# A two-layer decoder on one core: weight chunks split 1024 columns at a time, head outputs kept in DRAM

## The chip, the core and the metric

The kernel runs on one NeuronCore of a Trainium2 chip, as one program. The metric is the device time of one execution in microseconds, as the median of several runs. The core's engines are TensorE (PE in the profile, its weight loads PEld), VectorE (DVE), ScalarE (ACT), GpSimd (POOL) and SyncE (SP). Each works through its own instructions in a fixed order and waits on semaphores for the others. Here SP, ScalarE and POOL also issue DMA transfers, each on its own queue.

## The reference

Two pre-norm residual layers over 512 tokens of 2048 features, all in float32. Layer 0 projects its normed input to 12288 columns, runs two recurrences (RG-LRU, 8 heads of 256; HGRN2, 16 heads of 128), gates both, and maps the 4096 joined features back to 2048. Layer 1 is differential attention with 8 heads (two causal softmax maps each), again between two projections.

```python
h = rms_norm(x, rec_norm)
rg_x, rg_g, hg_q, hg_f, hg_i, hg_g = split(h @ rec_w_in)       # 2048 -> 6 x 2048
y_a = rg_lru(conv(rg_x), ...) * silu(rg_g)
y_b = rms_norm(hgrn2(silu(hg_q), hg_f, hg_i), hg_out_norm) * silu(hg_g)
x = x + concat(y_a, y_b) @ rec_w_out                           # 4096 -> 2048
h = rms_norm(x, att_norm)
q, k, v, g = split(h @ att_w_in)                               # 2048 -> 4 x 2048
o = rms_norm(diff_attention(rope(rms_norm(q)), rope(rms_norm(k)), v, lam))
x = x + (o * (1 - lam_init) * silu(g)) @ att_w_out             # 2048 -> 2048
```

## The kernel before, in words

**Products.** TensorE multiplies in a float32r format that holds only part of a float32. So each operand is split exactly into a high part (a rounding copy) and a low part (the rest), and each product is made as three: high·high, high·low, low·high (`mm3`, L104 to L106 before). A product takes 128 x 128 weights against 512 moving columns.

**Weights.** They come in chunks of [128, 1024] float32 (512 KB): 192 of `w_rec`, 8 of `w_gate`, 64 of `w_rout`, 128 of `w_att`, 32 of `w_aout`. `raw` loads a chunk into one of three buffers `wraw` on SP's queue (L84). `split` makes `whi` with a ScalarE cast (L91) and `wlo` with a VectorE subtract (L92), 512 columns at a time, in five buffers each. Splits have high priority in the scheduler, which otherwise orders each engine's instructions by data flow. A chunk feeds 24 products of 512 columns.

**Stages.** `proj_feat` projects 256 features per job (4 chunks, two PSUM banks `pj` out of four), `proj_tok` 512 features per job (four banks). First come the HGRN2 jobs, two heads at a time, then the RG-LRU jobs, then the output projection (4 blocks of 16 chunks, HGRN2's y16 to y31 first and y0 to y15 after them), then attention (4 pairs of heads, with jobs q, k, v, g of 8 chunks each) and the last output projection (4 blocks of 8 chunks). The heads' own work is written as generators, and `tick` takes some steps of it between two half chunks of a projection.

**Head outputs.** They stay in SBUF as tiles `yb0` to `yb7`, `ya0` to `ya15` and, in layer 1, `y0` to `y15`. For each block of the output projections `jit_split` splits each of them anew, 512 columns at a time, in the same `whi` and `wlo`.

**Start.** `run` loads x transposed in eight pairs of tiles into `yb0` to `yb7` on SP's queue, three weight chunks among them; ScalarE and VectorE make `h0h`, `h0l` and so on from them (L744, L745). `prepare` loads x again in eight tiles on POOL's queue (L165), in turns through `yb5`, `yb6`, `yb7`, and ScalarE squares them and sums the squares (L166). From the sums comes 1/rms of each token, which TensorE turns into a row (`pm<-cst,xr`, L182) that ScalarE copies to `rrow` (L183). VectorE multiplies each finished projection bank by it (`hin<-pj,rrow`, L384), which frees the bank.

Of the kernel before, what the change touches and what calls it, by code (L numbers as in the profile page):

```python
# [9 lines left out]
F32 = mybir.dt.float32  # L10
# [9 lines left out]
P = 128  # L20
# [15 lines left out]
# steps of the heads' own work between two half chunks of a projection  # L36
# [10 lines left out]
# columns of the packed constants  # L47
# [4 lines left out]
class Kernel:  # L52
# [27 lines left out]
    def raw(self, src):  # L80
        if self.raws and self.use_raws:
            return self.raws.pop(0)
        t = self.wp.tile([P, CH], F32, name="wraw", bufs=3)
        self.nc.sync.dma_start(t, src)  # L84
# [23 lines left out]
    def rsqrt(self, pool, ss, n, scale, eps):  # L108
        """(ss * scale + eps) ** -0.5 on a few columns"""
# [7 lines left out]
        # first guess from the bits, then Newton until float32 has converged  # L117
# [8 lines left out]
    def proj_feat(self, h, src, chunk0, ticks):  # L126
        """256 output features as two [feature, token] banks"""
        ps = [self.pj.tile([P, S], F32, name="pj") for _ in range(2)]
        for c in range(4):
            raw = self.raw(src[chunk0 + c])  # L130
            for s in range(2):
                w = self.split(raw[:, s * HALF:(s + 1) * HALF])
                for kk in range(2):
                    kt = 4 * c + 2 * s + kk
                    for o in range(2):
                        sl = slice(kk * 256 + o * P, kk * 256 + (o + 1) * P)
# [4 lines left out]
    def proj_tok(self, lhs, order, src, chunk0, ticks):  # L141
        """512 output features as four [token, feature] banks; lhs(kt) gives the split activations"""
        ps = [self.pj.tile([P, S], F32, name="pj") for _ in range(NT)]
        n = len(order)
        for c in range(n // 2):
            raw = self.raw(src[chunk0 + c])
            for s in range(2):
                i = 2 * c + s
                w = self.split(raw[:, s * HALF:(s + 1) * HALF])
# [7 lines left out]
    def prepare(self):  # L157
        """1 / rms of each token, as columns and as a row repeated for every partition; small constants"""
# [3 lines left out]
        for i in range(8):  # L162
            xt = self.ybp.tile([P, 2 * S], F32, name=f"yb{5 + i % 3}")
# [47 lines left out]
        # the scale of q goes with k  # L211
# [709 lines left out]
```

## Time and profile before

| | |
|---|---|
| median of 3 runs | 2596.66 us (2596.36 to 2597.73) |
| profiled execution: span from the first to the last instruction | 2594.6 us |
| mean granted TensorE clock | 0.998 |
| L91 casts, 128x512, of weight chunks | x848, mean 618 ns |
| L92 subtracts, 128x512, of weight chunks | x848, mean 688 ns |
| HBM read, written | 239.95 MB, 8.39 MB |

The span of the profiled execution lies 2.06 us under the median of the runs; a device time of its own is not listed for it. In a row of groups, "out<-in" names tiles, "x" a count; a bracket [t <-X] in a timeline says that the engine was idle for t us and that X ended it. An instruction's time is from its start to its modelled end, so back-to-back products, which start some 0.225 us apart, show as 0.39 us each.

### The profile page before, as it was taken

The numbers are of one execution on the slowest core, as the hardware profiler recorded it, in microseconds if no ns is written. First come the engines' busy times: TensorE is split into PE (matmuls) and PEld (weight loads), VectorE is DVE, ScalarE is ACT, GpSimd is POOL, SyncE is SP. The second block draws the span as 40 slices with busy tenths as digits, with TensorE's granted clock in tenths as the row PEclk, the third lists the DMA queues.
The fourth block names the chain that finished last, engine by engine and source line by source line (L and its number), as shares of the span: only waits on it lengthen the run. The fifth ranks groups of instructions, "written<-read, shape, count | busy, mean of one in ns | idle before, by whom it ended". The sixth has DMA issues, their size and how long they took to land.

```text
span 2594.6 us, 33221 instructions
## 1 busy us (share of the span) xinstructions
PE 2579.6 (99%) x12416; PEld 2126.2 (82%) x12416; DVE 1417.0 (55%) x3073; ACT 1258.6 (49%) x2458; POOL 4.6 (0%) x12
## 2 busy tenths in 40 slices
PE   9999999999999999999999999999999999999999
PEld 7888888888888888888888888888888888888887
DVE  5466557646646665545654555344544534544654
ACT  8445545535444455556544444334434434534543
POOL 0000000000000000000000000000000000000000
PEclk9999999999999999999999999999999999999999
DMA  6222222222222222222232333222222222222243
GB/s 244 96 74 82 81 82 74 81 90 74 76 95 74 74 98 102 97 93 98 90 128 95 127 130 120 98 98 75 81 97 77 79 91 82 76 95 93 86 146 114
DMA packets 73457, 250.48 MB, mean 97 GB/s; under 512 B 8144, under 2 KB 8656, under 8 KB 73296
## 3 DMA queue, kind: packets, MB, share of 16 engines
q1 hardware_dynamic: 71712, 243.58, 26.8%
q0 software_dynamic: 1152, 4.19, 0.4%
q8 instruction: 97, 1.59, 0.2%
q10 hardware_dynamic: 432, 0.59, 0.1%
q14 instruction: 64, 0.52, 0.1%
HBM read 239.95 MB, written 8.39 MB: 96 GB/s over the span
## 4 chain that ended last, share of the span: by engine, by line
PE 94%; DVE 2%; ACT 2%; DMA 1%; issue 1%; SPq 0%; ACTq 0%
PE pj L104 28%; PE pj L106 28%; PE pj L105 28%; PE pm L258 2%; PE pm L570 1%; PE pm L104 1%; PE pm L106 1%; PE pm L105 1%; PE pm L343 1%; PE pm L554 1%; DMA yb<-in_x 0%; PE pm L332 0%; PE pm L345 0%; ACT a L675 0%; PE pm L359 0%
## 5 line engine op out<-in xcount | busy, mean ns | idle before, releaser
L92 DVE TENSOR_TENSOR wlo<-wraw,whi 128x512 fp32r<-128x512 f32 x848 | 582.3, 688 | 671.4 <-ACT whi L91 641.2
L91 ACT CAST whi<-wraw 128x512 fp32r<-128x512 f32 x848 | 523.0, 618 | 765.0 <-PE pj L106 463.7
L106 PE MATMUL pj<-whi,wlo 128*128 128x512 f32 x768 | 299.6, 390 | 0.0
L105 PE MATMUL pj<-wlo,whi 128*128 128x512 f32 x768 | 299.4, 390 | 0.0
L104 PE MATMUL pj<-whi 128*128 128x512 f32 x768 | 299.3, 390 | 0.0
L106 PEld LDWEIGHTS pj<-whi,wlo 128*128 128x128 f32 x768 | 144.2, 188 | 30.5 <-DVE wlo L92 0.6
L104 PEld LDWEIGHTS pj<-whi 128*128 128x128 f32 x768 | 144.2, 188 | 30.4 <-issue 0.5
L105 PEld LDWEIGHTS pj<-wlo,whi 128*128 128x128 f32 x768 | 144.2, 188 | 29.1
L240 ACT ACTIVATE e<-e 128x512 f32<-128x512 f32 x80 | 50.5, 632 | 131.7 <-DVE e L239 97.6
L92 DVE TENSOR_TENSOR wlo<-ya,whi 128x512 fp32r<-128x512 f32 x64 | 44.3, 693 | 89.9 <-ACT whi L91 89.9
L92 DVE TENSOR_TENSOR wlo<-y,whi 128x512 fp32r<-128x512 f32 x64 | 44.2, 691 | 82.3 <-ACT whi L91 82.3
L91 ACT CAST whi<-ya 128x512 fp32r<-128x512 f32 x64 | 39.7, 621 | 100.9 <-PE pj L105 100.9
L91 ACT CAST whi<-y 128x512 fp32r<-128x512 f32 x64 | 39.9, 623 | 94.1 <-PE pj L105 90.2
L92 DVE TENSOR_TENSOR wlo<-yb,whi 128x512 fp32r<-128x512 f32 x64 | 44.1, 690 | 72.2 <-ACT whi L91 72.0
L91 ACT CAST whi<-yb 128x512 fp32r<-128x512 f32 x64 | 39.8, 621 | 76.5 <-PE pj L105 76.5
L258 PEld LDWEIGHTS pm<-e 128*128 128x128 f32 x512 | 66.6, 191 | 5.0 <-DVE e L241 0.3
L258 PE MATMUL pm<-e 128*128 128x128 f32 x512 | 67.5, 275 | 0.0
L241 DVE TENSOR_TENSOR e<-e,hin 128x256 f32<-128x256 f32 x80 | 33.6, 420 | 58.8 <-ACT e L240 58.8
L575 ACT ACTIVATE p<-pm,mx 128x128 f32<-128x128 f32 (+3 forms) x64 | 33.7, 526 | 40.6 <-DVE mx L573 38.6
L572 DVE TENSOR_REDUCE mx<-pm 128x1 f32<-128x128 f32 (+3 forms) x64 | 30.4, 485 | 32.6 <-PE pm L571 32.3
L675 ACT ACTIVATE a<-pj,rstd 128x128 f32<-128x128 f32 x128 | 47.3, 421 | 0.3
L104 PE MATMUL pj<-h0h,whi 128*128 128x512 f32 x80 | 33.8, 423 | 5.2 <-DVE hin L384 2.9
(474 smaller groups left out, 6483.0 us busy)
## 6 DMA issues: line engine op xcount, KB each, us to landing
wraw<-in_w_rec SPq DMA_DIRECT2D x192, 512.0 KB, 3.2
wraw<-in_w_att SPq DMA_DIRECT2D x128, 512.0 KB, 3.2
wraw<-in_w_rout SPq DMA_DIRECT2D x64, 512.0 KB, 3.2
wraw<-in_w_aout SPq DMA_DIRECT2D x32, 512.0 KB, 3.2
yb<-in_xT SPq DMA_DIRECT2D x8, 512.0 KB, 8.5
yb<-in_x POOLq DMA_DIRECT2D x8, 512.0 KB, 5.5
wraw<-in_w_gate SPq DMA_DIRECT2D x8, 512.0 KB, 3.2
xo<-in_x SPq DMA_DIRECT2D x16, 256.0 KB, 4.0
```

What stands on the lines that cost most here:

```text
L91: self.nc.scalar.copy(hi, src)
L92: self.nc.vector.tensor_tensor(lo, src, hi.bitcast(F32), op=ALU.subtract)
L104: mm(out, a[0], b[0], start=start, stop=False)
L105: mm(out, a[0], b[1], start=False, stop=False)
L106: mm(out, a[1], b[0], start=False, stop=stop)
L240: nc.scalar.activation(e, e, AF.Exp)
L241: V.tensor_tensor(e1, e1, vw(qs, h)[:, :, 1, :], op=ALU.mult)
L258: nc.tensor.matmul(ps[:, sl], e[:, sl], e[:, sl], start=True, stop=True)
L343: nc.tensor.matmul(po[:, sl], st[:, sl], v[:, t, vc:vc + P], start=True, stop=t == 0)
L572: V.tensor_reduce(mx[:, i:i + 1], ps[:, :n], axis=AX.X, op=ALU.max)
L575: nc.scalar.activation(e[:, :n], ps[:, :n], AF.Exp, scale=ATT_SCALE, bias=mx[:, i:i + 1], accum_out=z[:, i:i + 1])
L675: nc.scalar.activation(x[:, t, g * P:(g + 1) * P], ps[t][:, g * P:(g + 1) * P], AF.Square, scale=r1, accum_out=ss[:, t * 4 + g:t * 4 + g + 1])
```

## The change

Weight chunks are split whole, 1024 columns by one cast and one subtract. The split tiles double in size, with three buffers (`WBUFS`) in place of five, and raw chunks have two (`RBUFS`) in place of three. Head outputs are written as pairs of feature tiles [128, 2, 512] to DRAM by a DMA on ScalarE's queue (`keep_y`), and each block of an output projection reads each pair back on SP's queue (`y_split`), splits it 1024 columns wide, and uses the two halves. The tiles of `yb` become one name with eight buffers that are taken in turn, by `prepare` as well. At the start two weight chunks are loaded among the x tiles instead of three. The scratch tile `jk3` becomes bfloat16. Comments and docstrings are dropped, so line numbers move a little. Core of the diff:

```diff
+RBUFS, WBUFS, YBUFS = 2, 3, 2
...
-        t = self.wp.tile([P, CH], F32, name="wraw", bufs=3)
+        t = self.wp.tile([P, CH], F32, name="wraw", bufs=RBUFS)
...
-    def split(self, src):
-        hi = self.wp.tile([P, HALF], F32R, name="whi", bufs=5)
-        lo = self.wp.tile([P, HALF], F32R, name="wlo", bufs=5)
+    def split(self, src, pool, name, bufs):
+        hi = pool.tile([P, CH], F32R, name=name + "hi", bufs=bufs)
+        lo = pool.tile([P, CH], F32R, name=name + "lo", bufs=bufs)
...
-            raw = self.raw(src[chunk0 + c])
+            wh, wl = self.split(self.raw(src[chunk0 + c]), self.wp, "w", WBUFS)
             for s in range(2):
                 i = 2 * c + s
-                w = self.split(raw[:, s * HALF:(s + 1) * HALF])
+                w = [x[:, s * HALF:(s + 1) * HALF] for x in (wh, wl)]
...
-            xt = self.ybp.tile([P, 2 * S], F32, name=f"yb{5 + i % 3}")
+            xt = self.ybp.tile([P, 2 * S], F32, name="yb", bufs=8)
...
-        self.y[16 + hd] = y
+        if hd % 2:
+            self.keep_y(8 + hd // 2, self.yb)
...
-                y = self.y1p.tile([P, S], F32, name=f"y{kt}")
-                nc.scalar.activation(y, ps, AF.Identity, scale=self.gsub[:, fb:fb + 1])
-                self.y[kt] = y
+                if fb == 0:
+                    y = self.y1p.tile([P, 2, S], F32, name="ya", bufs=2)
+                nc.scalar.activation(y[:, fb, :], ps, AF.Identity, scale=self.gsub[:, fb:fb + 1])
+                if fb:
+                    self.keep_y(2 * pr + hh, y)
...
-    def jit_split(self, kt):
-        return self.split(self.y[kt])
+    def keep_y(self, i, y):
+        d = self.dr.tile([P, 2 * S], F32, name=f"yd{i}")
+        self.nc.scalar.dma_start(d, y.rearrange("p a c -> p (a c)"))
+        self.y[i] = d
+
+    def y_split(self):
+        at = [None, None]
+        def lhs(kt):
+            i = kt // 2
+            if at[0] != i:
+                if i not in self.y:
+                    self.drain()
+                t = self.yp.tile([P, CH], F32, name="yraw", bufs=2)
+                self.nc.sync.dma_start(t, self.y[i])
+                at[:] = i, self.split(t, self.yp, "y", YBUFS)
+            sl = slice(kt % 2 * S, (kt % 2 + 1) * S)
+            return at[1][0][:, sl], at[1][1][:, sl]
+        return lhs
...
-                if i % 2 == 0 and i < 6:
+                if i % 2 == 0 and i < 2 * RBUFS:
                     self.raws.append(self.raw(self.w_rec[i // 2]))
...
-                ps = self.proj_tok(lhs, order, self.w_rout, 16 * n, 1)
+                ps = self.proj_tok(self.y_split(), order, self.w_rout, 16 * n, 1)
```

At the start of the program SP issued its loads like this before; the third `wraw` is the third weight chunk, and the eight `yb` loads are the pairs of x tiles:

```order
L730 DMA yb_132<-in_xT 128x1024
L734 DMA col<-in_col 128x163
L84 DMA wraw<-in_w_rec 128x1024
L730 DMA yb_138<-in_xT 128x1024
L730 DMA yb_140<-in_xT 128x1024
L84 DMA wraw<-in_w_rec 128x1024
L730 DMA yb_144<-in_xT 128x1024
L730 DMA yb_146<-in_xT 128x1024
L84 DMA wraw<-in_w_rec 128x1024
L730 DMA yb_150<-in_xT 128x1024
```

And like this now, with equal rows counted:

```order
L756 DMA yb<-in_xT 128x1024
L760 DMA col<-in_col 128x163
L86 DMA wraw<-in_w_rec 128x1024
L756 DMA yb<-in_xT 128x1024 x2
L86 DMA wraw<-in_w_rec 128x1024
L756 DMA yb<-in_xT 128x1024 x5
L764 DMA cst<-in_cst 128x384
L86 DMA wraw<-in_w_rec 128x1024 x135
```

The third weight chunk has moved from between the fifth and the sixth pair of x tiles to behind the eighth and the constants.

On ScalarE the casts of that chunk stood between the h tiles before (h8h is the first tile that needs it):

```order
L744 ACTIVATE h8h<-yb_146,col 128x512
L744 ACTIVATE h9h<-yb_146,col 128x512
L91 CAST whi<-wraw 128x512 x2
L744 ACTIVATE h10h<-yb_150,col 128x512
L744 ACTIVATE h11h<-yb_150,col 128x512
```

Now its one cast stands behind the last of them, ahead of the first square of x:

```order
L770 ACTIVATE h12h<-yb,col 128x512
L770 ACTIVATE h13h<-yb,col 128x512
L206 ACT_TABLE_LOAD
L770 ACTIVATE h14h<-yb,col 128x512
L770 ACTIVATE h15h<-yb,col 128x512
L93 CAST whi<-wraw 128x1024
L167 ACTIVATE yb,ss_336<-yb 128x1024
```

At the end of the attention, ScalarE before: `pm` holds the transposes of the last head, y14 and y15 are its outputs, and the casts of y12 to y15 are the last of the first block:

```order
L91 CAST whi_20669<-wraw_20667 128x512
L626 ACTIVATE y14_20596<-pm_20591,gsub_527 128x512
L626 ACTIVATE y15_20603<-pm_20598,gsub_527 128x512
L91 CAST whi_20673<-y12_20383 128x512
L91 CAST whi_20689<-wraw_20667 128x512
L91 CAST whi_20693<-y13_20390 128x512
L91 CAST whi_20711<-wraw_20709 128x512
L91 CAST whi_20715<-y14_20596 128x512
```

And now: `ya_18916` is the pair of the last head, `yd7` its place in DRAM, `yraw_19016` what comes back of it:

```order
L93 CAST yhi_18982<-yraw_18980 128x1024
L93 CAST whi_19012<-wraw_19010 128x1024
L632 ACTIVATE ya_18916<-pm_18911,gsub_495 128x512
L632 ACTIVATE ya_18916<-pm_18918,gsub_495 128x512
L704 DMA yd7_18924<-ya_18916 128x1024
L93 CAST whi_19065<-wraw_19063 128x1024
L93 CAST yhi_19018<-yraw_19016 128x1024
```

A store and a load have come between the last head's outputs and their cast.

More of the change, by code (lines that the diff above doesn't have):

```diff
@@ L129, in proj_feat @@
         for c in range(4):
-            raw = self.raw(src[chunk0 + c])
+            w = self.split(self.raw(src[chunk0 + c]), self.wp, "w", WBUFS)
             for s in range(2):
-                w = self.split(raw[:, s * HALF:(s + 1) * HALF])
                 for kk in range(2):
@@ L135, in proj_feat @@
                     for o in range(2):
-                        sl = slice(kk * 256 + o * P, kk * 256 + (o + 1) * P)
+                        sl = slice(s * HALF + kk * 256 + o * P, s * HALF + kk * 256 + (o + 1) * P)
                         self.mm3(ps[o], (w[0][:, sl], w[1][:, sl]), h[kt], kt == 0, kt == KD - 1)
@@ L145, in proj_tok @@
         for c in range(n // 2):
-            raw = self.raw(src[chunk0 + c])
+            wh, wl = self.split(self.raw(src[chunk0 + c]), self.wp, "w", WBUFS)
             for s in range(2):
                 i = 2 * c + s
-                w = self.split(raw[:, s * HALF:(s + 1) * HALF])
+                w = [x[:, s * HALF:(s + 1) * HALF] for x in (wh, wl)]
                 a = lhs(order[i])
@@ L360, in hgrn_head @@
         if hd % 2 == 0:
-            self.yb = self.ybp.tile([P, 2, S], F32, name=f"yb{hd // 2}")
+            self.yb = self.ybp.tile([P, 2, S], F32, name="yb", bufs=8)
         y = self.yb[:, hd % 2, :]
         V.scalar_tensor_tensor(y, ps, self.col[:, C_HGN:C_HGN + 1], sg, op0=ALU.mult, op1=ALU.mult)
-        self.y[16 + hd] = y
+        if hd % 2:
+            self.keep_y(8 + hd // 2, self.yb)
         yield
@@ L448, in rg_head @@
             xs.append((hi, lo))
-            w.append(self.split(wg[:, ct * HALF:(ct + 1) * HALF]))
+            if ct == 0:
+                wh, wl = self.split(wg, self.wp, "w", WBUFS)
+            w.append([x[:, ct * HALF:(ct + 1) * HALF] for x in (wh, wl)])
             yield
@@ L487, in rg_head @@
             V.tensor_tensor_scan(m, a[jt], m, 0.0, op0=ALU.mult, op1=ALU.add)
-            y = self.yap.tile([P, S], F32, name=f"ya{c}")
-            V.tensor_tensor(y, m, sg[jt], op=ALU.mult)
-            self.y[c] = y
+            if jt == 0:
+                y = self.yap.tile([P, 2, S], F32, name="ya", bufs=2)
+            V.tensor_tensor(y[:, jt, :], m, sg[jt], op=ALU.mult)
+            if jt:
+                self.keep_y(hd, y)
             yield
@@ L728, in run @@
             for i in range(8):
-                t = self.ybp.tile([P, 2, S], F32, name=f"yb{i}")
+                t = self.ybp.tile([P, 2, S], F32, name="yb", bufs=8)
                 nc.sync.dma_start(t, self.xT[:, 2 * i:2 * i + 2, :])
@@ L761, in run @@
             self.rk = pool(st, "rk")
+            self.yp = pool(st, "yp")
             self.mids.append(m)
@@ L770, in run @@
             for n in range(4):
-                def lhs(kt):
-                    if kt not in self.y:
-                        self.drain()
-                    return self.jit_split(kt)
-                ps = self.proj_tok(lhs, order, self.w_rout, 16 * n, 1)
+                ps = self.proj_tok(self.y_split(), order, self.w_rout, 16 * n, 1)
                 xo = []
@@ L781, in run @@
                     nc.sync.dma_start(x1d[t, n], o)
-                    jk = self.ev.tile([P, S], F32, name="jk3", bufs=1)
+                    jk = self.ev.tile([P, S], BF16, name="jk3", bufs=1)
                     nc.scalar.activation(jk, o, AF.Square, accum_out=ss1[:, t, n:n + 1])
@@ L816, in run @@
             V.tensor_scalar(self.nlam, self.nlam, -LAM_INIT, None, op0=ALU.add)
+            self.yp = pool(st, "yp")
             self.attention(h1)
             for n in range(4):
-                def lhs(kt):
-                    if kt not in self.y:
-                        self.drain()
-                    return self.jit_split(kt)
-                ps = self.proj_tok(lhs, list(range(KD)), self.w_aout, 8 * n, TICK_OUT)
+                ps = self.proj_tok(self.y_split(), list(range(KD)), self.w_aout, 8 * n, TICK_OUT)
                 xo = self.ak.tile([P, NT, S], F32, name="a0")
```

1 line of the change is left out of this document (removed).

## The prediction

> **What bounds the kernel now.** I read the busy times and the chain that ended last first, then TensorE's waits, then windows by stage, and at last the timeline of the first 60 us. In the rows of busy times each engine has its microseconds, its share of the span and its instructions.
>
> ```profile
> span 2594.6 us, 33221 instructions
> PE 2579.6 (99%) x12416; PEld 2126.2 (82%) x12416; DVE 1417.0 (55%) x3073; ACT 1258.6 (49%) x2458; POOL 4.6 (0%) x12
> ...
> PE 94%; DVE 2%; ACT 2%; DMA 1%; issue 1%; SPq 0%; ACTq 0%
> ```
>
> TensorE is busy for 2579.6 of 2594.6 us, so 15 us are idle in all. VectorE and ScalarE have half of their time free; what the change saves or adds there reaches the end only where a product waits for it. TensorE's waits (line, released by: us in total, times, longest) say where that is:
>
> ```profile
> PE pj L104 <- DVE hin L384: 3.2, 2, 2.9
> PE pj L104 <- ACT whi L91: 2.2, 1, 2.2
> PE pm L359 <- DVE kp L354: 1.5, 9, 0.3
> ```
>
> Splits (whi, wlo) hold up TensorE once, for 2.2 us, at the start. There is next to nothing to win by cheaper splits, so the question is which new waits the change makes. The windows (us; busy time and instructions of PE, PEld, DVE, ACT, POOL; granted clock; DMA share; GB/s) show the places of loss and two undisturbed stages, the first output projection and the last:
>
> ```profile
> 8.00:12.00 4.00, 4.00 (x11) 3.13 (x12) 2.62 (x5) 3.97 (x7) 0.00 (x0) 0.57 1.00 401
> 53.00:57.00 4.00, 1.07 (x7) 0.71 (x6) 2.27 (x5) 3.95 (x5) 0.00 (x0) 0.88 0.34 131
> 57.00:63.00 6.00, 6.00 (x15) 4.67 (x16) 1.93 (x4) 2.89 (x6) 0.00 (x0) 0.51 0.01 3
> 1350.00:1420.00 70.00, 70.00 (x311) 57.98 (x310) 34.16 (x53) 29.60 (x52) 0.00 (x0) 1.00 0.31 109
> 2460.00:2530.00 70.00, 70.00 (x310) 57.75 (x309) 37.25 (x59) 29.41 (x52) 0.00 (x0) 1.00 0.46 158
> ```
>
> After the two stops (at 8 us and at 57 us) the granted clock is 0.57 over 4 us and 0.51 over 6 us: 1.7 and 2.9 us of work are lost there beyond the stops themselves. Elsewhere it is 1.00.
>
> **The start.** Here the change matters most.
>
> ```profile
> 7.33 1.14 ACT L91 CAST whi<-wraw 128x512 fp32r<-128x512 f32 x2 [0.33 <-DMA wraw<-in_w_rec]
> 7.98 1.29 DVE L92 TENSOR_TENSOR wlo<-wraw,whi 128x512 fp32r<-128x512 f32 x2
> 8.00 0.57 PE L104 MATMUL pj<-h0h,whi 128*128 128x512 f32 x1 [2.24 <-ACT whi L91]
> 20.61 0.39 PE L104 MATMUL pj<-h8h,whi 128*128 128x512 f32 x1
> 22.93 0.71 ACT L744 ACTIVATE h15h<-yb,col 128x512 fp32r<-128x512 f32 x1
> 27.04 1.06 ACT L166 ACTIVATE yb<-yb 128x1024 f32<-128x1024 f32 x1
> ```
>
> (1) The first product waits for a cast of 1024 columns instead of one of 512. The nearest 1024-wide ScalarE row is L166, 1.06 us; so TensorE starts at 7.33 + 1.06 + 0.05 = 8.44 instead of 8.00: **+0.44**. The subtract behind it (1.29 for both halves now) is wanted only by the fifth product and is hidden by the four before.
>
> (2) The third weight chunk. With two raw buffers its load moves on SP's queue from ahead of the fifth pair of x tiles to behind the last pair and the constants. These are issues from the timeline (start, us) and, in windows that hold one or two of them, their KB and us to landing: first the third chunk, then the last x pair, then two that left on two queues at the same time, and last the median of all w_rec chunks:
>
> ```profile
> 5.78 0.49 SPq L84 DMA_DIRECT2D wraw<-in_w_rec  x1
> ...
> 8.62 0.33 SPq L730 DMA_DIRECT2D yb<-in_xT  x1
> ...
> 30.71 0.53 POOL L165 DMA_DIRECT2D yb<-in_x  x1 [1.71 <-ACT yb L166]
> ...
> wraw<-in_w_rec SPq DMA_DIRECT2D x1, 512.0 KB, 9.2
> ...
> yb<-in_xT SPq DMA_DIRECT2D x1, 512.0 KB, 10.2
> ...
> wraw<-in_w_rec SPq DMA_DIRECT2D x1, 512.0 KB, 6.6
> yb<-in_x POOLq DMA_DIRECT2D x1, 512.0 KB, 6.9
> ...
> wraw<-in_w_rec SPq DMA_DIRECT2D x192, 512.0 KB, 3.2
> ```
>
> The third chunk landed at 5.78 + 9.2 = 15.0; the last x pair, three loads behind it, at 8.62 + 10.2 = 18.8: one load per 1.28 us. Moved behind the three pairs and the constants (some 0.5 us) it lands at 15.0 + 3 × 1.28 + 0.5 = 19.4, if SP's queue had the DMA engines to itself. It does not: with yb as one name of eight buffers the loads of x on POOL's queue reuse the first buffers, and are freed by the first splits of h instead of the sixth pair.
>
> ```profile
> 7.08 0.75 DVE L745 SCALAR_TENSOR_TENSOR h1l<-yb,col,h1h 128x512 fp32r<-128x512 f32 x1
> ...
> 11.32 0.74 DVE L745 SCALAR_TENSOR_TENSOR h3l<-yb,col,h3h 128x512 fp32r<-128x512 f32 x1
> 12.65 0.74 DVE L745 SCALAR_TENSOR_TENSOR h5l<-yb,col,h5h 128x512 fp32r<-128x512 f32 x1
> ...
> 21.29 0.66 POOL L165 DMA_DIRECT2D yb<-in_x  x1 [20.85 <-DVE lm_a L421]
> ```
>
> Before, POOL's first load left at 21.29; now it can leave at 7.83, the second at 12.06, the third at 13.39. Two loads in flight on two queues took 6.6 and 6.9 us where one alone takes 3.2, so they share about evenly. From 12 us POOL always has one to send. Between 7.8 and 19.4 SP has 11.6 us of transfers left; shared evenly throughout, as many again go between: that would end near 30. But each load of x needs a split of h that itself needs an x pair further up in SP's queue, so I count 5.5 of them ahead of the third chunk: 19.4 + 5.5 × 1.28 = 26.5. TensorE wants it at 20.61 + 0.44 = 21.05 and gets it at 26.5 + 1.06 + 0.05 = 27.6: **+6.6**. Bounds: ScalarE's row puts this cast behind h15's (22.93, now some 0.5 earlier, since the cast no longer stands ahead of it), so even a chunk that lands at 19.4 is cast at 22.4 + 0.6 and used at 24.1: +3.1, or +2.5 with a faster run of ScalarE; at 30 it is +10. Later chunks have 5.4 us of products each, 24 that start 0.225 apart, against 1.28 to 2.56 per load: no more stalls there.
>
> (3) The clock behind this stop. The stop of 2.93 us at 53.85 was followed by the window at 0.51, which lost 2.9; the first one lost 1.7. I take **+2.9** (1.7 to 3.0), since the stop is long like that one or longer. [...]
>
> (4) The wait for rrow.
>
> ```profile
> 53.25 0.60 PE L182 MATMUL pm<-cst,xr 128*128 128x128 f32 x4
> 54.77 0.62 ACT L91 CAST whi<-wraw 128x512 fp32r<-128x512 f32 x1
> 55.30 0.58 ACT L183 COPY rrow<-pm 128x512 f32<-128x512 f32 x1
> 55.42 0.69 DVE L92 TENSOR_TENSOR wlo<-wraw,whi 128x512 fp32r<-128x512 f32 x1 [1.24 <-ACT whi L91]
> 56.04 0.69 DVE L384 TENSOR_TENSOR hin<-pj,rrow 128x512 f32<-128x512 f32 x1
> 56.78 0.80 PE L104 MATMUL pj<-h0h,whi 128*128 128x512 f32 x1 [2.93 <-DVE hin L384]
> ```
>
> The eleventh chunk's cast still stands ahead of the copy of rrow and, with three split buffers, waits for the last product of the eighth (about 53.4, on the old clock). Then cast 1.06, the subtract 1.28 ahead of hin on VectorE, hin 0.69: TensorE goes on near 56.45, a wait of 2.6 instead of 2.93. **−0.4**, with the slow clock behind it as before.
>
> **The stages in between: 0.** In a projection chunk k+3's split now waits for the end of chunk k; it is wanted 10.8 us later and takes 1.06 + 1.28 after a load of 3.2. In the output projections each pair of chunks moves 1 MB instead of 0.5: the DMA share of 0.31 and 0.46 becomes some 0.55 and 0.7; a y split waits for a buffer freed 5.4 us before its use and takes 2.4. VectorE's two halves took 1.29 for 1024 columns, ScalarE's 1.14 against 1.06: what is saved there lies beside products. If that cover went, each of 96 output chunks would pay some tenths (third rival). The heads' own waits (L359, 1.5 us in all) keep their chain: 0. ScalarE issues the 24 stores of y and then meets casts that wait for y's load; a block of about 2 us, covered by splits already made: **+0.5** (0 to 3).
>
> **The end of the attention.** The last head's y goes out to DRAM and in again between its transposes and its use in the first of the four last projections. On TensorE 47 products lie between, 47 × 0.225 = 10.6 us. These rows give the prices (the loads and stores in 2500 to 2550, and a store of the first layer):
>
> ```profile
> 2444.00 1.26 ACT L626 ACTIVATE y<-pm,gsub 128x512 f32<-128x512 f32 x2
> ...
> wraw<-in_w_aout SPq DMA_DIRECT2D x9, 512.0 KB, 3.4
> out<-a SPq DMA_DIRECT2D x8, 256.0 KB, 4.3
> a<-x1d SPq DMA_DIRECT2D x4, 256.0 KB, 4.8
> ...
> x1d<-xo SPq DMA_DIRECT2D x4, 256.0 KB, 5.6
> ```
>
> ScalarE is in two 1024-wide casts when the transposes end (1.6 us more), then evacuates y (1.26): 2.85. Store of 512 KB 4.3 to 5.6, load 3.4 to 4.8, cast 1.06: the first product is possible 11.6 to 14.3 after the transposes, 1.0 to 3.7 late; the subtract (1.28) is wanted 0.45 after it: 0.8 more. So 1.8 to 4.5; if ScalarE's casts come sooner it is 0, and with a slow clock behind the stop 6 at most. I take 4.9 + 3.4, since a load of this size (3.4) is shown and the store is twice the one of 4.3: 12.2, 1.6 late, with the subtract **+2.4**. Before, y went from tile to cast and this was covered.
>
> **Sum.** 0.44 + 6.6 + 2.9 − 0.4 + 0.5 + 2.4 = +12.4 on the profiled span of 2594.6, that is 2607.0; the median of the runs, 2596.66, lies 2.1 above that span, which the profiled execution should share. Forecast 2609.
>
> **Rivals.** (a) Faster: the early loads of x bring the sums of squares forward so that rrow is ready before its wait, and the third chunk comes in time. Then 2.93 of wait and 2.9 of slow clock go, and about 0.4 of start is paid: 2596.7 − 5.8 + 0.4 ≈ 2591. It decides if rrow's copy runs before 53.4. For it: the loads leave 13 us sooner. Against it: the copy stands behind a cast that waits for the end of the eighth chunk, and behind the transposes at 53.25. 0.08. (b) No change that can be told: POOL's loads hardly disturb, the stop is 2.5 to 3.1 and the clock loses little, and the last head's y is covered: 2596.7 + 0.44 + 2.5 − 0.4 + 0 to 2 = 2599 to 2601.5. Against it stands the pair 6.6/6.9; 0.15. (c) The DRAM round trips starve output chunks: SP's queue stands at a y load that waits for a buffer while the next weight load is behind it. At 0.3 us in 96 chunks it is +29 and 2638, at 0.1 +10 and 2619. It begins where a load lands later than 5.4 − 2.4 = 3.0 us after its buffer frees, and 3.2 to 3.4 is the price of one; against it, each load is issued one chunk earlier than that. 0.12.
>
> **Numbers.** The forecast (the sum, 2602 to 2617) has 0.65. Range 2598.5 to 2617.5: it takes in (b) and the upper bounds of (2) and of the last head together in part, and leaves out (a) and most of (c). About 0.2% (5.2 us) is what a measurement can tell from no change. Faster 0.08 (a); same 0.16 ((b) and the forecast's lower edge); slower 0.76.
>
> **What would show it.** TensorE's first product at 8.4; a wait of 5 to 9 us on whi before h8's product, ended by the third chunk's landing near 26 and followed by a granted clock of 0.5; POOL's first load near 7.9; hin's wait about 2.6; 70 us without idle in both output stages; one wait of 1 to 4 us before the last head's product. Wrong, if the third chunk lands before 22, or if waits on whi or yhi appear at every chunk of the output stages.

## The result, and the profile after

The changed kernel takes 2619.41 us (2618.95 to 2619.51) against 2596.51 in the same series: +22.9 us, a ratio of 1.0088 with a 95% interval of 1.0073 to 1.0102. The forecast was 2609, with a range up to 2617.5: +12.4 us, about half of what came. The sign was right, the size was not.

The head of the page after, its chain that ended last, and TensorE's two largest waits (us in total, times, longest):

```profile
span 2617.6 us, 31949 instructions
PE 2599.5 (99%) x12416; PEld 2128.0 (81%) x12416; DVE 1368.4 (52%) x2553; ACT 1203.5 (46%) x1953; POOL 4.6 (0%) x12
...
PE 96%; DVE 1%; DMA 1%; ACT 1%; issue 0%; SPq 0%; DVEq 0%; ACTq 0%
...
PE pj L106 <- ACT whi L93: 6.1, 2, 4.8
PE pj L106 <- DVE hin L386: 2.3, 1, 2.3
```

TensorE's idle time rose from 15.0 to 18.1 us only. The other 20 us are in its busy time, with the same 12416 products: they ran longer, some of them under a slow clock, most of them not. The windows after, at places that answer to those shown of before:

```profile
24.00:30.00 6.00, 4.07 (x10) 3.20 (x11) 4.56 (x13) 4.62 (x7) 0.53 (x1) 0.50 1.02 406
63.36:70.66 7.30, 7.00 (x24) 5.58 (x25) 3.28 (x6) 5.83 (x8) 0.00 (x0) 0.77 0.23 74
1350.00:1420.00 70.00, 70.00 (x310) 56.55 (x309) 34.34 (x33) 28.90 (x36) 0.00 (x0) 1.00 0.65 212
2460.00:2530.00 70.00, 69.69 (x303) 55.95 (x302) 36.04 (x40) 25.70 (x27) 0.00 (x0) 1.00 0.71 232
```

A slow clock follows the stop at the start (0.50 over 6 us, of which TensorE stood still for 1.9) and the wait for hin (0.77 over 7.3 us, 1.7 us lost). In the output projections next to no time is idle (0.3 of 70 us in the last) and the clock is 1.00. Yet the products there are longer. These rows group one of the three products by stage (count: shortest/median/longest in ns, first and last start): first the kernel before, then after, each in the first output projection and in the last.

```profile
L104 PE MATMUL pj<-whi x484: 387/389/485, 1259.8 to 1599.8; 128*128 128x512 f32 x162
L104 PE MATMUL pj<-whi x118: 389/389/421, 2500.0 to 2579.7; 128*128 128x512 f32 x118
```

```profile
L106 PE MATMUL pj<-whi,yhi x471: 393/394/482, 1259.6 to 1599.8; 128*128 128x512 f32 x157
L106 PE MATMUL pj<-whi,yhi x114: 395/396/396, 2500.2 to 2579.3; 128*128 128x512 f32 x114
```

Even the shortest product after is longer than the median before: it is not some of them that wait, but all. From start to start (the pitch) they take 233.3 ns on average in both output projections, most of them 231 and 236 in the first and 232 and 235 in the last, where the kernel before takes 227.

The first product of certain chunks in TensorE's row, us from the span's start, shows where the 23.0 us of the span come from:

| first product of | before | after | later by | gained in this stretch |
|---|---|---|---|---|
| fifth chunk (first stop over) | 31.5 | 39.0 | 7.5 | start 7.5 |
| tenth chunk | 65.2 | 70.9 | 5.7 | wait for hin and its slow clock −1.8 |
| first output projection | 1249.6 | 1257.5 | 7.9 | HGRN2, RG-LRU 2.2 |
| attention | 1610.2 | 1628.9 | 18.7 | 10.8 |
| last output projection | 2400.1 | 2418.8 | 18.7 | 0.0 |
| last product | 2590.3 | 2613.4 | 23.1 | 4.4 |

The two output projections, forecast at 0 and +2.4, hold 15.2 us. The rows of the start after, on four engines:

```profile
8.34 0.66 POOL L166 DMA_DIRECT2D yb<-in_x  x1 [7.90 <-DVE h1l L771]
9.32 0.33 SPq L86 DMA_DIRECT2D wraw<-in_w_rec  x1
24.84 1.04 ACT L93 CAST whi<-wraw 128x1024 fp32r<-128x1024 f32 x1 [2.95 <-DMA wraw<-in_w_rec]
25.93 0.79 PE L106 MATMUL pj<-h8h,whi 128*128 128x512 f32 x1 [4.81 <-ACT whi L93]
33.53 0.39 PE L106 MATMUL pj<-h12h,whi 128*128 128x512 f32 x1
```

The third chunk, issued at 9.32, is cast at 24.84 with ScalarE waiting for its landing, and TensorE has waited 4.81 us. The last row is the first product of the fourth chunk.

### The profile page after: what moved, and what is told of

The parts are those of the page before. It is cut to its first block, busy times and chain, and to the rows that moved or that the text cites. A ratio compares the mean times of both kernels' runs of the same rounds, so it can differ in the third digit from the quotient of the medians.

```text
span 2617.6 us, 31949 instructions
## 1 busy us (share of the span) xinstructions
PE 2599.5 (99%) x12416; PEld 2128.0 (81%) x12416; DVE 1368.4 (52%) x2553; ACT 1203.5 (46%) x1953; POOL 4.6 (0%) x12
## 4 chain that ended last, share of the span: by engine, by line
PE 96%; DVE 1%; DMA 1%; ACT 1%; issue 0%; SPq 0%; DVEq 0%; ACTq 0%
PE pj L106 29%; PE pj L108 28%; PE pj L107 28%; PE pm L259 2%; PE pm L576 1%; PE pm L106 1%; PE pm L108 1%; PE pm L107 1%; DMA wraw<-in_w_rec 1%; PE pm L344 1%; PE pm L333 1%; PE pm L560 0%; PE pm L346 0%; ACT a L682 0%; PE pm L360 0%; PE pm L319 0%
## 5 line engine op out<-in xcount | busy, mean ns | idle before, releaser
L94 DVE TENSOR_TENSOR wlo<-wraw,whi 128x1024 fp32r<-128x1024 f32 x424 | 518.2, 1222 | 570.5 <-ACT whi L93 569.1
L93 ACT CAST whi<-wraw 128x1024 fp32r<-128x1024 f32 x424 | 444.8, 1049 | 647.8 <-PE pj L108 384.2
L106 PE MATMUL pj<-whi,yhi 128*128 128x512 f32 x768 | 304.1, 396 | 0.0
L107 PE MATMUL pj<-wlo,yhi 128*128 128x512 f32 x768 | 304.1, 396 | 0.0
L108 PE MATMUL pj<-whi,ylo 128*128 128x512 f32 x768 | 303.8, 396 | 0.0
L94 DVE TENSOR_TENSOR ylo<-yraw,yhi 128x1024 fp32r<-128x1024 f32 x96 | 117.6, 1225 | 263.5 <-ACT yhi L93 263.5
L93 ACT CAST yhi<-yraw 128x1024 fp32r<-128x1024 f32 x96 | 100.6, 1048 | 285.9 <-PE pj L107 275.1
L108 PEld LDWEIGHTS pj<-whi,ylo 128*128 128x128 f32 x768 | 144.4, 188 | 34.6
L106 PEld LDWEIGHTS pj<-whi,yhi 128*128 128x128 f32 x768 | 144.4, 188 | 34.2
L107 PEld LDWEIGHTS pj<-wlo,yhi 128*128 128x128 f32 x768 | 144.4, 188 | 33.9
```

Source lines behind the costliest of these rows:

```text
L93: self.nc.scalar.copy(hi, src)
L94: self.nc.vector.tensor_tensor(lo, src, hi.bitcast(F32), op=ALU.subtract)
L106: mm(out, a[0], b[0], start=start, stop=False)
L107: mm(out, a[0], b[1], start=False, stop=False)
L108: mm(out, a[1], b[0], start=False, stop=stop)
```

## Experiments on the slow products

Three explanations stood at first: the place of the split outputs in SBUF, the DMA traffic that had doubled, and the width of the tiles. In these products the split of y (yhi, ylo) is the weights, and the split of the weight chunk (whi, wlo) is the moving operand.

Behind each time stands its ratio to the kernel before in the same series, with the 95% interval; a single run has none. The kernel before lay at 2595.7 to 2596.7 us in these series. "Less than the changed kernel" compares with its 2619.41 us, from another series. The addresses are the places that the built program gives the tiles; a trace does not hold them.

**The pool moved down.** One line is moved in each stage:

```diff
+            self.yp = pool(st, "yp")
             self.ev = pool(st, "ev")
             self.yap = pool(st, "yap")
             self.rk = pool(st, "rk")
-            self.yp = pool(st, "yp")
...
             self.y1p = pool(st, "y1p")
+            self.yp = pool(st, "yp")
             self.ak = pool(st, "ak")
...
-            self.yp = pool(st, "yp")
             self.attention(h1)
```

> The changed kernel with one difference: the pool of yraw, yhi and ylo is opened ahead of the other pools of its stage, so that the split outputs lie at bytes 170528 to 186912 of a partition in the first output projection and 135648 to 152032 in the last, instead of 208384 to 224800. Loads, splits and the order of the products' operands stay. Theory A (place): a product whose weights come from the upper end of SBUF starts the next one 231 to 236 ns later instead of 227. Moved down, all 2304 of them are back at 227; that is 10.2 us less in the first output projection and 4.4 less in the last: 2604 to 2606. Theory B (traffic): the doubled loads slow TensorE's reads; then the pitch stays at 231 to 236 and the time at 2618 to 2621. Theory C (width: a slice of a tile 1024 columns wide as weights is slower): as B.

It took 2615.35 us, 1.0074 (1.0059 to 1.0089). The first output projection stayed slow, the last is as before the change:

```profile
L106 PE MATMUL pj<-whi,yhi x471: 393/394/482, 1259.8 to 1600.0; 128*128 128x512 f32 x157
L106 PE MATMUL pj<-whi,yhi x119: 388/389/390, 2499.8 to 2580.0; 128*128 128x512 f32 x119
```

In the last stage neither traffic (DMA share 0.71 in 2500 to 2570 us, in the changed kernel 0.68) nor width had changed, only the place: so traffic and width are out as the cause there, and place in some sense is in.

**An eighth of the bytes.** Of each pair only an eighth of the columns is loaded; the rest of the head outputs is left out of both output projections and set to 1.

```diff
-                self.nc.sync.dma_start(t, self.y[i])
+                self.nc.sync.dma_start(t[:, :128], self.y[i][:, :128])
+                self.nc.gpsimd.memset(t[:, 128:], 1.0)
```

> The changed kernel with an eighth of the bytes that come back from DRAM: of each yraw only the first 128 columns are loaded, the rest is set to 1 by GpSimd (so seven eighths of the head outputs are left out of both output projections). Places in SBUF, widths and the order of the splits stay. Theory A (place): the pitch of the products with y stays at 231 to 236 ns and the time within 3 us of 2619. Theory B (traffic): the DMA share in the output projections falls from 0.67 to about 0.4 and the pitch to 227; 2604 to 2607. Theory C (width): as A.

One run, 2619.76 us. The DMA share fell to 0.41, in 1300 to 1370 us from 0.67 and in 2500 to 2570 us from 0.68; the products did not move (394, 396):

```profile
1300.00:1370.00 70.00, 70.00 (x309) 56.61 (x309) 37.82 (x37) 28.93 (x36) 10.91 (x13) 1.00 0.41 140
...
L106 PE MATMUL pj<-whi,yhi x470: 393/394/482, 1260.0 to 1599.5; 128*128 128x512 f32 x157
L106 PE MATMUL pj<-whi,yhi x115: 395/396/397, 2499.9 to 2579.7; 128*128 128x512 f32 x115
```

Traffic is out in both stages.

**Split outputs in the yb buffers.** These are free when the first output projection begins. For the last one the pool stays low, as in the run with the pool moved down.

```diff
+    def ytile(self, dt):
+        self.yc += 1
+        return self.ybp.tile([P, 2, S], dt, name="yb", bufs=8).rearrange("p a c -> p (a c)")
...
-                t = self.yp.tile([P, CH], F32, name="yraw", bufs=2)
+                t = self.yp.tile([P, CH], F32, name="yraw", bufs=2) if self.yp else self.ytile(F32)
```

> The changed kernel with yraw, yhi and ylo of the first output projection in the eight yb buffers (bytes 121312 to 154080), which are free by then, and with those of the last one at 127456 to 152032 as in the run before. That run left them at 170528 to 186912 in the first output projection, where the pitch stayed at 231 to 236, and at 127456 to 152032 in the last, where it fell to 227. If the place decides (by its own address, or by its distance from the moving operand at 29152 to 53728), both stages now run at 227: 10 us less in the first, 4.4 in the last, 2604 to 2606. If something else of the first output projection makes it slow (ScalarE's and VectorE's other work, the order of the blocks), it stays at 231 to 236 there and the time at 2614 to 2616.

It took 2604.35 us, 1.0034 (1.0022 to 1.0046), 15 us less than the changed kernel; both stages are at 389 ns:

```profile
L107 PE MATMUL pj<-whi,yb x483: 389/389/481, 1260.2 to 1599.4; 128*128 128x512 f32 x161
L107 PE MATMUL pj<-whi,yhi x119: 389/389/390, 2499.7 to 2579.9; 128*128 128x512 f32 x119
```

So the traffic, the width and the round trip through DRAM are all still there (DMA share 0.67 in 1300 to 1370 us, as in the changed kernel), and the output projections are as fast as before.

**Distance or address?** The pool of h goes ahead of the weights' pool:

```diff
-        self.wp = pool(ctx, "wp")
         self.hp = pool(ctx, "hp")
+        self.wp = pool(ctx, "wp")
```

> The changed kernel with the pool of h placed ahead of the weights' pool: whi now lies at 94688 to 106976 and wlo at 106976 to 119264, instead of 29152 and 41440; yhi and ylo stay at 208384 to 224800. Distance theory: a product is slow when the weights that are loaded beside it lie more than about 120 to 128 KB from its moving operand; the distance is now at most 122 KB (it was 127 KB and more in the slow stages, 123 KB at most in the fast one), so the products with y are at 227 and the time 2604 to 2607. Address theory: weights that lie above some address between 152032 and 170528 are slow, wherever the moving operand lies: 231 to 236, 2618 to 2621.

It took 2619.14 us, 1.0090 (1.0076 to 1.0104); the products stayed slow in both output projections (233.3 ns from start to start). The distance theory fell. The address theory fell with the next run.

**An edge?** Here the first output projection has yhi and ylo at 162336 to 178720, the last at 152032 to 168416 (raw pairs elsewhere), by the order of the pools.

```diff
+            self.yp = pool(st, "yp")
             self.ev = pool(st, "ev")
...
             self.y1p = pool(st, "y1p")
+            self.ak2 = pool(st, "ak2")
+            self.yp = pool(st, "yp")
             self.ak = pool(st, "ak")
```

> Where the slow place begins. As the run with y splits in the yb buffers, but yhi and ylo lie at 162336 to 178720 in the first output projection and at 152032 to 168416 in the last (raw pairs in yb and below 152032). By the runs so far weights that end below 154080 are at 227 and those above 170528 at 231 to 236. If there is an edge, products whose weights lie below it show 227 and those above it 231 to 236, in both stages at the same address: an edge at 160 KB (163840) would leave yhi of the last projection fast and nearly all else slow. If it is a gradual thing or depends on the stage, the same address has two pitches in the two stages. Time 2606 to 2618, by the share that is slow.

One run, 2615.32 us. The addresses 162336 to 168416 occur in both stages. They were slow in the first and fast in the last:

```profile
L108 PE MATMUL pj<-whi,yhi x470: 393/394/483, 1260.0 to 1599.5; 128*128 128x512 f32 x157
...
L108 PE MATMUL pj<-whi,yhi x118: 389/389/389, 2500.0 to 2579.6; 128*128 128x512 f32 x118
```

No edge then. What the fast places had in common was only seen in the low bits of the addresses that the pools give. That made a fourth theory: the weights' tile and the moving operand's must have the same address modulo some power of two.

**Pads of a few bytes.** Nothing but an unused tile ahead of yraw, of 64 and 224 bytes of a partition in the two stages (448 and 480 in the second run):

```diff
             self.yp = pool(st, "yp")
+            nc.vector.memset(self.yp.tile([P, 16], F32, name="pad"), 0.0)
...
             self.yp = pool(st, "yp")
+            nc.vector.memset(self.yp.tile([P, 56], F32, name="pad"), 0.0)
             self.attention(h1)
```

> The changed kernel with nothing but a pad ahead of yraw in its pool: 64 bytes of a partition in the first output projection, 224 in the last. The place stays at the upper end; what changes is the address of yhi and ylo modulo small powers of two. All whi, wlo and h tiles lie at 480 modulo 512. In all slow stages so far y lay at 32 or 0 modulo 128 (208416, 208384, 170528, 162336), in all fast ones at 96 like the moving operand (yb 121312 and on, 135648, 152032). The pad puts y at 96 modulo 128 and modulo 512 in the first projection, and at 96 modulo 128 and 224 modulo 256 and 512 in the last. Alignment theory, modulus 128: both stages at 227, 2604 to 2606. Modulus 256: the first slow, the last at 227, 2614 to 2616. Modulus 512 or more: both slow, 2618 to 2621, as by any theory of place in the large.

> As the run with the small pads, but 448 and 480 bytes: y at 480 modulo 512 (2016 modulo 2048) in both output projections, at the upper end of SBUF. Alignment theory with a modulus up to 512: both stages at 227, 2603 to 2607. Modulus 2048: both slow, 2618 to 2621.

The small pads gave 2614.67 us, 1.0069 (1.0052 to 1.0086), the larger ones 2605.96 in one run. Small pads first, then larger ones:

```profile
L106 PE MATMUL pj<-whi,yhi x472: 390/393/479, 1260.0 to 1599.9; 128*128 128x512 f32 x158
L106 PE MATMUL pj<-whi,yhi x118: 389/389/389, 2500.2 to 2579.8; 128*128 128x512 f32 x118
```

```profile
L106 PE MATMUL pj<-whi,yhi x484: 389/389/476, 1259.9 to 1599.9; 128*128 128x512 f32 x162
L106 PE MATMUL pj<-whi,yhi x118: 389/389/389, 2500.2 to 2579.8; 128*128 128x512 f32 x118
```

In one run, 448 and 480 bytes of pad took 13.5 us from the changed kernel. The runs fit a modulus of 256: a difference of 128 bytes is slow (small pads, first output projection, 232.6 ns from start to start), one of 256 is fast (small pads, last one, 227.0).

**Everything moved by 64.** A pad of 64 bytes in the first pool of all (`cp`).

> The changed kernel with 64 bytes of pad at the very start, so that all tiles behind it move up by 64 together: whi, wlo and h from 96 to 32 modulo 128, yhi and ylo from 32 to 96 (first projection) and from 0 to 64 (last). Their distances stay. Relative theory (what matters is that weights and moving operand have the same address modulo the modulus): nothing changes, products with h 227, products with y 231 to 236, 2617 to 2621. Absolute theory (96 modulo 128 is the good place of weights): products with y in the first projection fall to 227, but all products with h and w in the other stages rise to 231 to 236, some 7700 of them by 6.5 ns: 2655 to 2665.

One run, 2618.77 us; products with y stayed slow (median 394 ns in the first output projection, 396 in the last), the others stayed as before (389). At this shift it is the difference of the two addresses that counts, not each by itself.

All these runs in one table; the difference is yhi less whi, modulo 256 bytes, and the pitch the mean from start to start of the products of the stage, stretches over 300 ns left out:

| run | first output projection: difference, ns | last: difference, ns |
|---|---|---|
| before (y splits in whi, wlo) | 0, 227.0 | 0, 227.2 |
| after | 64, 233.3 | 32, 233.3 |
| pool moved down | 64, 233.3 | 0, 227.1 |
| an eighth of the bytes | 64, 233.3 | 32, 233.3 |
| yb buffers | 0, 226.9 | 0, 227.0 |
| h first | 64, 233.3 | 32, 233.3 |
| edge | 64, 233.3 | 0, 227.0 |
| small pads | 128, 232.6 | 0, 227.0 |
| larger pads | 0, 226.9 | 0, 227.1 |
| all moved by 64 | 64, 233.3 | 32, 233.3 |

**The kernel before, made slow.** The last test takes nothing of the change but the cause that was found, an offset between the two operands:

```diff
         self.hp = pool(ctx, "hp")
+        self.nc.vector.memset(self.hp.tile([P, 16], F32, name="pad"), 0.0)
```

> The kernel before, with nothing but a pad of 64 bytes of a partition ahead of the h tiles: h lies 64 bytes beside whi and wlo modulo 256, where it was equal before; y splits stay in whi and wlo. Alignment theory: in the projections from h, 192 and 128 chunks of 24 products, the pitch rises from 227 to 231 to 236 (6.5 ns more), 7680 products, 50 us: 2640 to 2650, while both output projections stay at 227. If it is something of the changed kernel's y tiles (another dtype of buffer, another pool, a DMA as their source), the pad changes nothing: 2595 to 2598.

It took 2618.35 us, 1.0083 (1.0066 to 1.0100): 64 unused bytes cost the kernel before 21.8 us, nearly as much as the whole change did. In the attention's projections, where h is the weights (kernel before, then with the pad):

```profile
L105 PE MATMUL pj<-wlo,h5h x60: 387/389/398, 1669.4 to 2365.9; 128*128 128x512 f32 x60
```

```profile
L105 PE MATMUL pj<-wlo,h5h x60: 392/394/398, 1678.7 to 2388.2; 128*128 128x512 f32 x60
```

The attention took 15.0 us more for its 3072 products, 4.9 ns each; why that is less than the 6.3 of the output projections is open. In the HGRN2 stage the 768 products of the value projections, where h is the weights too, took 4.3 us more. Both output projections took what they took before (360.7 us from the first one's start to the attention's). But the 3840 products of the feature projections, where whi and wlo are the weights and h moves, took only 3.9 us more: there the weights lie 192 bytes ahead modulo 256 and not 64, and the pitch rose by 1 ns on average. The expected 50 us were too high by that. So the size of the penalty depends on more than equal or unequal: 6.3 ns at a difference of 32 or 64, 5.6 at 128, 1 at 192, the last with the roles of the two splits exchanged. Why is not shown.

The slow pitch was the same, 233.3 ns, at a DMA share of 0.41 and of 0.67. In the output projections 6.3 of these ns hang on the difference of the two addresses, by whatever mechanism.

## Experiments on the start

**The loads of x late again**: the yb tiles have their own names as before.

```diff
-            xt = self.ybp.tile([P, 2 * S], F32, name="yb", bufs=8)
+            xt = self.ybp.tile([P, 2 * S], F32, name=f"yb{5 + i % 3}")
```

> The changed kernel with the yb tiles named one by one as before, so that the loads of x on GpSimd's queue go through yb5, yb6 and yb7 and leave after h11l instead of after h1l. The third weight chunk stays behind the last pair of x tiles on SP's queue. Sharing theory (the early loads of x push it back): it lands near 19.5 instead of 24.8, its cast stands behind h15's at 21.2 to 21.9, the wait of 4.8 us for it falls to 1.5 to 2.5 and the slow clock behind it loses 0 to 2 less: 2613 to 2617. Queue theory (its place behind the x pairs alone makes it late): it lands at 23 or later, 2618 to 2620. The place theory says nothing on it: the products with y stay at 231 to 236 ns.

It took 2615.96 us, 1.0075 (1.0060 to 1.0090), 3.5 less than the changed kernel; the interval overlaps with the changed kernel's, so the gain is read from the trace, where the fifth chunk starts at 35.2 and not at 39.0. The third chunk landed at 18.7 instead of 24.8, as the sharing theory had it, and its cast then waited for ScalarE's row:

```profile
22.67 0.79 PE L106 MATMUL pj<-h8h,whi 128*128 128x512 f32 x1 [3.42 <-ACT whi L93]
```

**The third chunk early**: its load ahead of the last two x pairs, once the first chunk is split.

```diff
+                if i == 5:
+                    w0 = self.raws[0]
+                    self.early[id(w0)] = self.split(w0, self.wp, "w", WBUFS)
+                    self.raws.append(self.raw(self.w_rec[2]))
```

> The changed kernel with the third weight chunk's load ahead of the last two pairs of x tiles and the constants on SP's queue; the loads of x stay early. The issue waits for the first chunk's split (near 9.3) with the DMA engines still busy on earlier loads. Queue theory: the chunk lands two pairs, the constants and the loads of x that ran between them earlier, at 18 to 20.5 instead of 24.8; its cast stands ahead of h12's, the wait of 4.8 us is 0 to 0.5 and the slow clock behind it goes: 2611 to 2614, 5 to 8 less. Sharing theory (the loads of x alone make it late): it lands 3 us earlier at most and the time is 2616 to 2618. Either way the products with y stay at 231 to 236 ns.

It took 2615.56 us, 1.0073 (1.0056 to 1.0090), 3.9 less where 5 to 8 were expected, again with intervals that overlap; in the trace the fifth chunk starts at 36.5. The third chunk landed at 17.7 and its wait was gone. But the fourth chunk now landed at 27.2, behind the same loads of x, and the stop came one chunk later:

```profile
28.42 0.80 PE L109 MATMUL pj<-h12h,whi 128*128 128x512 f32 x1 [3.45 <-ACT whi L96]
```

So both causes were there, the loads of x that leave early and the third chunk's place behind the x pairs, each alone sufficient for a stop of 3.4 us with a slow clock behind it (with x late 0.84 over 24 to 30 us, with the third chunk early 0.68 over 30 to 36).

**All mends**: both of these, the y splits of the first output projection in the yb buffers, and those of the last low.

> All mends together: y splits in the yb buffers and low in the last projection, yb tiles named one by one (the loads of x leave late) and the third weight chunk ahead of the last two pairs of x tiles. Each of the two mends of the start alone moved the stop to the next place (ScalarE's row behind h15h; the fourth chunk). Together: the third chunk lands near 16 and the fourth near 19, no stop there, the fifth chunk starts at 31.5 to 33 as before the change instead of 39; 6 to 7.5 us less, and 14.6 less in the output projections: 2596 to 2600, no change against the kernel before that can be told. If the early stop turns up a third time elsewhere: 2601 to 2605.

It took 2597.74 us, 1.0007 (0.9998 to 1.0016): no change against the kernel before that can be told. Against the run with the yb buffers in the same series, the two mends of the start are worth 6.6 us. Its two largest waits, and the stretch around the end of the wait for hin:

```profile
PE pj L110 <- DVE hin L390: 2.3, 1, 2.3
PE pj L110 <- ACT whi L97: 1.9, 1, 1.9
...
56.09:63.39 7.30, 7.00 (x31) 5.81 (x32) 3.27 (x6) 7.12 (x10) 0.00 (x0) 1.00 0.20 74
```

**Splits of 512 again**, in the same wide tiles, with all mends:

```diff
-            self.nc.scalar.copy(hi, src)
-            self.nc.vector.tensor_tensor(lo, src, hi.bitcast(F32), op=ALU.subtract)
+            for s in (slice(0, HALF), slice(HALF, CH)):
+                self.nc.scalar.copy(hi[:, s], src[:, s])
+                self.nc.vector.tensor_tensor(lo[:, s], src[:, s], hi[:, s].bitcast(F32), op=ALU.subtract)
```

> The run with all mends, but with each split made again as two casts and two subtracts of 512 columns in the same 1024-wide tiles: what the width alone is worth. ScalarE and VectorE are busy some 40 to 60 us longer each. If the width matters only for the first product, it starts 0.4 earlier and the rest is the same: within 2 us of that run. If fewer instructions on ScalarE and VectorE shorten waits of the heads' own work in the HGRN2 and RG-LRU stages (or the longer ones lengthen them, 2.9 us by the changed kernel's drift there), it is up to 3 us less or more.

It took 2598.75 us, 1.0009 (1.0001 to 1.0018): the same as with wide splits, within the intervals. The width of the splits is worth nothing that can be told here.

**Past both kernels.** The wait for hin was still there in the run with all mends: its row was ready at 48.0 and transposed at 53.5. Two steps of pause are taken out, in that run and in the kernel before:

```diff
         V.tensor_copy(rep.rearrange("p (a c) -> p a c", a=NT), r.unsqueeze(2).broadcast_to([P, NT, P]))
-        yield
-        yield
```

> The run with all mends, with the two steps of pause taken out that stand ahead of the transposes for rrow (the row was ready at 48.0 and the transposes ran at 53.5). The transposes run near 50.8, rrow is copied before the eighth chunk ends, and hin's wait of 2.3 us at 53.9 goes. If no other wait takes its place: 2.0 to 2.6 us less than that run, 2594.5 to 2596; against the kernel before no change that can be told, or just faster. If TensorE now waits for the row instead: the same as that run.

> The kernel before with the same two steps taken out, nothing else: its row was ready at 49.2 and the transposes ran at 53.25. hin's wait of 2.93 us and the slow clock behind it (2.9) go: 5 to 6 us less, 2590 to 2592. If the wait only turns into one for the row or for a cast: 2593 to 2597.

With all mends it took 2594.08 us, 0.9992 (0.9983 to 1.0000); the kernel before with it 2592.84, 0.9988 (0.9979 to 0.9997), 3.2 us less than it was, not 5 to 6. With all mends the wait for hin is gone; in the kernel before one of 2.1 stayed, with a wait of 0.7 for the row and a clock of 0.72 behind it:

```profile
PE pj L104 <- DVE hin L382: 2.1, 1, 2.1
...
PE pm L180 <- DVE xr L177: 0.7, 1, 0.7
...
57.00:63.00 6.00, 6.00 (x21) 4.76 (x20) 2.52 (x4) 5.39 (x8) 0.00 (x0) 0.72 0.21 80
```

The interval of the first just reaches no change, that of the second does not; neither is clearly ahead of the other, and both are some 25 us under the changed kernel.

## Why the prediction was wrong, step by step

The step that failed is "The stages in between: 0", with the pitch of the products that the prediction took from the kernel before ("24 that start 0.225 apart") and never asked whether the change could touch it. The step priced loads, splits and buffers of the output projections, and these were hidden as it said (0.3 of 70 us idle at most). But the split outputs had moved from the weights' tiles to a pool of their own, whose address modulo 256 bytes differed from theirs, and each of 2304 products became some 6.3 ns longer: 14.5 us. The rival of starved output chunks named the right stages and, with +10 to +29, nearly the size, for another reason: there was no wait on yraw, whi or yhi in them, and the run with an eighth of the bytes moved nothing. That its lower end, 2619, is the measured time was luck.

- (1) +0.44 for the wider first cast: not to be told at the first product, which starts at 7.74, earlier than before, because the first weight chunk of this execution landed 4.9 us after its issue, not 5.7; in the profiled runs whose start is that of the changed kernel it starts at 7.6 to 8.7. The cast took 1.03 us as priced.
- (2) +6.6 for the third chunk: 4.8, mis-sized only. The chunk landed at 24.8, forecast 26.5, with four loads of x landed ahead of it and not 5.5; POOL's first load left at 8.34, forecast 7.83. In the other profiled runs with this start the wait was 5.2 to 6.3. Both single mends (landing at 18.7 and 17.7 instead of 24.8) and their sum showed the mechanism.
- (3) +2.9 for the clock: 2.2, within the bounds of 1.7 to 3.0. The clock was 0.50 over 6.83 us, but TensorE was still in its stop when that stretch began and was busy for only 4.37 of it:

```profile
23.47:30.30 6.83, 4.37 (x10) 3.47 (x11) 5.34 (x15) 4.92 (x7) 0.53 (x1) 0.50 1.03 408
```

So the third chunk's products took 7.6 us (25.93 to 33.53), where 24 of them take 5.4 at a clock of 1.00. That the clock would lose little behind a stop of 2.5 to 3.1, as in the rival of no change, no run shows: behind the stop of 3.4 with x late it was 0.87 over 18 to 24 us and 0.84 over 24 to 30.

- (4) −0.4 for hin: the wait was 2.3, forecast 2.6, and the slow clock behind it lost 1.7, where 2.9 had been lost before. That made −1.8. The prediction took the slow clock as fixed; the runs show that it is not. The same wait of 2.33 us was followed by a clock of 0.77 over 7.3 us in seven profiled runs (the changed kernel, the pool moved down, an eighth of the bytes, x late, the third chunk early, small and larger pads) and by 1.00 in four (yb buffers, h first, all mends, all moved by 64): 1.7 us that are lost in one run and not in another. In the changed kernel the slow stretch has sharp ends, and nine products instead of 16 fit into it:

```profile
61.02:64.43 3.41, 1.08 (x6) 0.73 (x5) 2.71 (x5) 3.28 (x5) 0.00 (x0) 1.00 0.14 25
64.43:67.85 3.42, 3.42 (x9) 2.65 (x9) 0.97 (x2) 3.37 (x5) 0.00 (x0) 0.50 0.35 133
67.85:71.26 3.41, 3.41 (x16) 2.79 (x15) 1.39 (x2) 1.91 (x3) 0.00 (x0) 1.00 0.00 0
```

The stretch behind the stop at the start is twice as long, 6.83 us. In the kernel before the slow stretches took the same lengths, 3.41 us (8.29 to 11.70) and 6.83 (56.07 to 62.90), and a loss of 1.7 is half of 3.41. Why the same wait is slow in one run and not in another is not shown; no run moved the wait on purpose. A wait of 2.33 was enough for a slow clock, 2.9 with the four transposes ahead of it.

- The stages from the tenth chunk to the first output projection: +2.2 instead of 0.5. They stayed with all mends (2.3) and with splits of 512 (2.9), so neither the start, the place of the y splits nor the width makes them; what they are is open.
- The end of the attention: +2.4 forecast, 0.0 measured up to the last projection and no wait after. ScalarE copied y out right behind the transposes (these end at 2462.81, the copies start at 2462.85), without the two casts that the forecast put in between at 1.6. The store of 512 KB was priced at 4.9 and took 2.9 from issue to landing, the load was priced at 3.4 and took 3.6. So the cast ended 9.0 us after the transposes, forecast 12.2, and 1.8 before its first product:

```profile
2464.14 0.33 ACTq L704 DMA_DIRECT2D yd<-ya  x1
...
2470.73 1.05 ACT L93 CAST yhi<-yraw 128x1024 fp32r<-128x1024 f32 x1 [1.48 <-DMA yraw<-yd]
...
2473.61 0.40 PE L106 MATMUL pj<-whi,yhi 128*128 128x512 f32 x1
...
yraw<-yd SPq DMA_DIRECT2D x3, 512.0 KB, 3.6
yd<-ya ACTq DMA_DIRECT2D x1, 512.0 KB, 2.9
```

Without the slow products the result would have been some +8 to +9 (22.9 less 14.5; the run with larger pads stands 9.2 above the kernel before of its series), so the rest of the sum was 4 too high: the last head and the start were each 2.4 too high and hin 1.4, against some 2 too low for the stages in between.

## What to carry to other kernels

Where a change moves an operand of TensorE to another pool, compare the pitch of the same products before and after, by their shortest and median time, before looking for waits: here they became 6.3 ns longer with at most 0.3 of 70 us idle. For float32r products like these, place the weights' and the moving operand's tiles at equal addresses modulo 256 bytes, as in all stages with y that ran at 226.9 to 227.2 ns here; pads of 448 and 480 bytes did it, and 64 bytes ahead of the h tiles undid it for the products with h. When one queue's load is late, ask which second cause stands ready to stop the same engine: here the two mends of the start gave 3.5 and 3.9 us alone and 6.6 together.

## What the runs showed that was not expected

- In the output projections a float32r product of 512 columns started its successor after 226.9 to 227.2 ns where the weights and the moving operand had equal addresses modulo 256 bytes, and after 232.6 to 233.3 where the weights lay 32, 64 or 128 bytes ahead. 64 bytes of pad made 21.8 us in the kernel before.
- The DMA share did not set the pitch. In 1300 to 1370 us it was slow at shares of 0.41 and 0.67 (an eighth of the bytes, after) and fast at 0.36 and 0.67 (before, yb buffers).
- A wait of TensorE as short as 2.33 us was followed by a slow clock (0.77 over 7.3 us) in seven profiled runs, which lost 1.7 us, and by 1.00 in four; in the kernel before without the two steps one of 2.1 was followed by 0.72 over 6 us. The loss does not follow the length: a wait of 2.9 us lost 2.9 (before), one of 4.8 lost 2.2 (after), one of 3.8 lost 1.7 (splits of 512).
